# A two-layer attention trunk: wider value products for eight heads, one weight loaded earlier, two more products of ones, and scores kept negated

## The chip, the cores and the metric

The kernel runs on one core of a Trainium2 chip. The metric is the device time of one execution in microseconds (us). The kernel before took 671.21 us, the median of three runs (671.16, 671.21 and 672.38).

## The reference, cut to what matters

Two layers work on 512 tokens of 1024 numbers. Layer 0 mixes tokens by neighbourhood attention: 16 heads of 64 numbers, where a token sees a window of 8 x 16 tokens of a 64-wide grid. Layer 1 is a latent attention over all tokens. After each layer a gated embedding is added. All numbers are float32.

```
def mixer_na(xn, w_in, rpb, w_out):
    q, k, v, z = jnp.split(xn @ w_in, 4, axis=-1)
    o = neighbourhood_attention(q.reshape(shp), k.reshape(shp), v.reshape(shp), rpb)
    return (o.reshape(B, S, hd) * jax.nn.silu(z)) @ w_out
...
for i in range(DEPTH):
    xn = rmsnorm(x, norm_g[i])
    y = mixer_na(...) if i == 0 else mixer_mla(...)
    h = x + y
    gate = jax.nn.sigmoid(rmsnorm(h, ple_norm[i]) @ ple_w_gate[i])
    x = h + gate * (p[i] @ ple_w_proj[i])
return rmsnorm(x, final_norm)
```

## The kernel before

**Precision.** Every product of two float32 matrices is made of three products of rounded halves: high by high, low by high, high by low. So each operand exists as a pair: `hi`, a rounded copy that ScalarE (ACT) makes, and `lo`, the difference, which VectorE (DVE) or GpSimd (POOL) makes. `load_w` (L68) does this for a weight of 128 x 1024 numbers (512 KB): a DMA from SyncE's queue (SP) into `wraw`, the cast to `whi` on ACT (L78), the subtraction to `wlo` on POOL (L79). Each of the three names has three buffers that rotate, so the third load behind a product waits until that product has read its weight.

**The order of the work.** The program is recorded in the order of the code, and a scheduler that simulates the engines then sets the order in which each engine issues. On the chip each engine takes its instructions strictly in that order. The PSUM banks have four tags: `mm` (2 banks), `S` (2), `T` (3) and `O` (1).

**The start (`run`, L752 to L799).** TensorE (PE) first multiplies a matrix of ones by ones, `NWARM` = 9 times (L756); nothing reads the result. Then come the 48 products of the embedding of layer 0 (`ple`, L430 and L102), whose operands `ple_load` casts in halves of 512 columns (L409, L410). The first two z projections (`z_phase` with `ws`, L173) follow; their weights and the transposed x (`xT`) were loaded above. They are made from x without its row norm (`rh`, `rl`). The norm comes from the four row tiles of x, which are loaded (L783) and squared (L784); POOL takes the power (L787), PE turns it into rows (four transposes into `ps_T`, L128), and ACT copies it to `R` (L792). The third z weight is the first that goes through `load_w` (L790), behind the x tiles and six writes of embedding results (L445) in SP's queue. From the norm and `xT` DVE makes the normed x (L796), and its halves `xh` and `xl` (L797, L798) are the operands of all that follows.

**The heads of layer 0 (`na_heads`).** `project(j)` makes queries and keys of a pair of heads; for even j it first makes the values of four heads (L220 to L233): two weights, then for each of four token tiles 24 products of 256 columns into one `mm` bank, which `v_split` divides. `attend(j)` runs the two heads of a pair (`na_head`): score products (L318, L319); on DVE score plus bias with the row maximum beside it (L325, L328); the negation of the maximum (L332, 128 x 2 numbers, 32 times in all); exponentials on ACT (L336); reciprocal on DVE; the division on POOL (L341); seven blocks turned on PE (L352, L354); and the product with the values (L366). `project(j + 1)` is recorded ahead of `attend(j)`. The last three z projections come after the heads (L291).

Of the kernel before, what the change touches and what calls it, by code (L numbers as in the profile page):

```python
# [27 lines left out]
QSC = 96.0 ** -0.5  # L28
NWARM = 9
NLATE = 3  # L30
# [9 lines left out]
class Trunk:  # L40
# [27 lines left out]
    def load_w(self, ap, n, extra=False, parts=1, rest=None, late=None):  # L68

        nc = self.nc  # L70
        pool = self.wx if extra else self.wp
        raw = self.wp.tile([P, 1024], F32, name="wraw", tag="wraw", bufs=3)
        hi = pool.tile([P, n if extra else 1024], F32R, name="whi", tag="whi", bufs=self.wxn if extra else 3)
        lo = pool.tile([P, n if extra else 1024], F32R, name="wlo", tag="wlo", bufs=self.wxn if extra else 3)
        w = n // parts
        for c in [slice(i * w, (i + 1) * w) for i in range(parts)]:
            nc.sync.dma_start(raw[:, c], ap[:, c])
            self.last_cast = nc.scalar.activation(hi[:, c], raw[:, c], AF.Copy)  # L78
            f = lambda e, c=c: e.tensor_tensor(out=lo[:, c], in0=raw[:, c], in1=hi[:, c].bitcast(F32), op=ALU.subtract)  # L79
# [133 lines left out]
    def na_heads(self, pool, xT, zs, oT):  # L213
# [3 lines left out]
        V, A, U = {}, {}, {}  # L217

        def project(j):
            if j % 2 == 0:  # L220
                g = j // 2
                wv = [self.load_w(a["na_v"][g, c], 1024, rest=nc.vector if g == c == 0 else None) for c in range(2)]
                vts = V[g] = []
# [55 lines left out]
        for i in range(2):  # L279
            la = pool.tile([P, S], F32R, name=f"la{i}", bufs=1)  # L280
            lb = pool.tile([P, S], F32R, name=f"lb{i}", bufs=1)
            nc.gpsimd.memset(la[64:128].bitcast(F32), 0.0)
            nc.gpsimd.memset(lb[0:64].bitcast(F32), 0.0)
            self.rest_k.append((la, lb))
        last = project(0)
        for j in range(8):
# [9 lines left out]
    def na_head(self, pool, h, sq, s0, dk, kl, vh):  # L296
# [9 lines left out]
        for half in range(2):  # L306
# [13 lines left out]
            for i in range(2):  # L320
                qt = 2 * half + i
                c = slice(qt, qt + 1)
                if qt == 0:
                    for r, sc in ((slice(0, 64), slice(0, 128)), (slice(64, 128), slice(128, 256))):
                        nc.vector.tensor_tensor_reduce(out=ex[r, 0:P], in0=sp[r, sc], in1=bias[r, 0:P], scale=1.0,  # L325
                                                       scalar=NEG, op0=ALU.add, op1=ALU.max, accum_out=mx[r, c])
# [5 lines left out]
            nc.vector.tensor_scalar(mx[:, hs], mx[:, hs], -1.0, None, op0=ALU.mult)  # L332
# [411 lines left out]
    def run(self):  # L744
# [7 lines left out]
        with tc.tile_pool(name="pre", bufs=4, reuse_waits="tile") as pool:  # L752
            ones = [nc.const_aps.tensor(1.0, (P, n), mybir.dt.bfloat16) for n in (P, S)]
            ps = self.psum("T")
            for i in range(NWARM):
# [33 lines left out]
            R = pool.tile([P, S], F32, name="R", bufs=1)  # L789
            first = self.load_w(a["na_z"][2], 1024)  # L790
            with tc.issue_after(self.last_cast.ins):
                nc.scalar.activation(R, turned, AF.Copy)  # L792
            zs = self.z_phase(a["na_z"], raw, range(2), R=R, ws=ws)
            for k in range(KD):
# [3 lines left out]
                (nc.vector, nc.gpsimd)[k % 2].tensor_tensor(out=lo, in0=xs[k], in1=hi.bitcast(F32), op=ALU.subtract)  # L798
            zs.update(self.z_phase(a["na_z"], raw, range(2, 8 - NLATE), R=R, first=first))  # L799
        oT = ([self.bigtile(f"oh{g}") for g in range(2)], [self.bigtile(f"ol{g}") for g in range(2)])  # L800
# [90 lines left out]
def layouts(i):  # L891
# [20 lines left out]
    f["na_z"] = c(tiles(w[:, 3072:], P).reshape(8, P, 1024))  # L912
    f["na_v"] = c(tiles(w[:, 2048:3072], 256).reshape(4, P, 2, 1024).transpose(0, 2, 1, 3))

    def rows(w):
        return c(tiles(w, S).reshape(2, P, 4, 1024).transpose(0, 2, 1, 3))

    f["na_o"] = rows(i["na_w_out"][0])
    f["mla_o"] = rows(i["mla_w_out"][0])
# [61 lines left out]
```

## Time and profile before

| what | value |
|---|---|
| runs, median | 671.21 us |
| the profiled execution's own time | 672.45 us |
| its span, first to last instruction | 670.6 us |
| PE busy | 660.7 us, 99% |
| DVE, ACT, POOL busy | 367.8, 407.0, 392.7 us |
| matmuls on PE | 3561 |

A profile is one execution. Its rows give the start of a group of instructions in us from the start of the span, the busy time of the group, the engine, the line, the tile written and the tiles read, the shapes, and how many instructions were merged. Matmuls overlap, so the duration of one (0.39 us, say) is longer than the distance between two starts; it is the distance that counts on a full PE. PEld is PE's loading of the stationary operand, which runs beside the products.

### The profile page before, as it was taken

Reading aid. Unit: us, or ns where it says so; the run is one execution under the profiler, and the core shown is the slowest. Engines: PE = TensorE matmul, PEld = TensorE weight load, DVE = VectorE, ACT = ScalarE, POOL = GpSimd, SP = SyncE. Lnnn points to the kernel's source line nnn. Section 1 sums busy time; section 2 is a strip of 40 time slices with the busy share of each in tenths; the row PEclk is TensorE's granted clock in tenths of the full one; section 3 lists DMA queues with packets and bytes.
Section 4 is the critical chain, followed back from the end, with each engine's and each line's share of the span. In section 5 each row is a group of like instructions: output and inputs, shape, how many; then the busy total and the mean of one; then the engine's idle time right before and its main releaser. Section 6 shows DMA issues by size and latency. Waiting matters only on the chain.

```text
span 670.6 us, 10167 instructions
## 1 busy us (share of the span) xinstructions
PE 660.7 (99%) x3561; PEld 565.6 (84%) x3561; DVE 367.8 (55%) x827; ACT 407.0 (61%) x812; POOL 392.7 (59%) x321
## 2 busy tenths in 40 slices
PE   9999999999999999999999999999999999999995
PEld 6789898998988888888899887888888888888885
DVE  6371464646747624453624613888988875145234
ACT  6663765657767652653444535887989887436423
POOL 0295546666575565853044526786959786758411
PEclk9999999999999999999999999999999999999999
DMA  8843314223233127534143344120111222664122
GB/s 322 308 154 133 107 56 138 88 65 115 67 96 118 44 101 290 189 123 129 72 118 109 104 110 132 66 74 16 58 47 63 64 96 95 241 244 156 34 79 94
DMA packets 32387, 79.11 MB, mean 118 GB/s; under 512 B 4177, under 2 KB 8785, under 8 KB 32337
## 3 DMA queue, kind: packets, MB, share of 16 engines
q1 hardware_dynamic: 31904, 77.68, 35.1%
q10 hardware_dynamic: 432, 0.79, 0.3%
q8 instruction: 28, 0.46, 0.3%
q14 instruction: 23, 0.18, 0.1%
HBM read 66.92 MB, written 8.39 MB: 112 GB/s over the span
## 4 chain that ended last, share of the span: by engine, by line
PE 88%; DMA 5%; ACT 2%; DVE 2%; POOL 1%; issue 1%; SPq 0%; POOLq 0%; DVEq 0%; ACTq 0%
PE ps_mm L102 50%; PE ps_S L102 11%; PE ps_mm L534 6%; PE ps_T L128 6%; PE ps_O L645 4%; PE ps_T L102 3%; PE ps_O L102 2%; PE ps_O L366 2%; PE ps_T L354 1%; DMA wraw<-na_z 1%; PE ps_S L319 1%; PE ps_S L318 1%; DMA x<-x 1%; DMA wraw<-proj 1%; DMA xT<-xT 1%
## 5 line engine op out<-in xcount | busy, mean ns | idle before, releaser
L79 POOL TENSOR_TENSOR wlo<-wraw,whi 128x1024 fp32r<-128x1024 f32 (+5 forms) x106 | 207.7, 1976 | 103.5 <-ACT whi L78 85.2
L78 ACT ACTIVATE whi<-wraw 128x1024 fp32r<-128x1024 f32 (+5 forms) x108 | 93.2, 886 | 73.7 <-issue 18.1
L630 POOL TENSOR_TENSOR ex<-ex,rc 128x512 f32<-128x512 f32 x64 | 66.0, 1039 | 25.9 <-DVE rc L629 16.7
L102 PE MATMUL ps_mm<-whi,hnT 128*128 128x512 f32 (+1 forms) x272 | 70.2, 378 | 0.0
L102 PEld LDWEIGHTS ps_mm<-whi,hnT 128*128 128x128 f32 x272 | 49.3, 188 | 9.3
L341 POOL TENSOR_TENSOR ex<-ex,rc 128x128 f32<-128x128 f32 (+1 forms) x64 | 34.3, 560 | 38.0 <-DVE rc L337 36.4
L628 ACT ACTIVATE ex<-ps_S,mx 128x512 f32<-128x512 f32 x64 | 44.0, 688 | 12.5 <-DVE mx L626 11.3
L626 DVE TENSOR_REDUCE mx<-ps_S 128x1 f32<-128x512 f32 x64 | 43.7, 683 | 8.7 <-PE ps_S L102 7.9
L91 DVE TENSOR_TENSOR pt_lo<-ps_T,pt_hi 128x512 fp32r<-128x512 f32 x64 | 43.3, 682 | 7.6 <-ACT pt_hi L89 7.3
L336 ACT ACTIVATE ex<-ex,mx 128x128 f32<-128x128 f32 (+1 forms) x64 | 30.2, 473 | 21.8 <-DVE mx L332 21.4
L102 PE MATMUL ps_mm<-xh,whi 128*128 128x512 f32 x152 | 41.0, 400 | 0.1
L102 PE MATMUL ps_mm<-wlo,hnT 128*128 128x512 f32 (+1 forms) x136 | 40.5, 378 | 0.0
L89 ACT ACTIVATE pt_hi<-ps_T 128x512 fp32r<-128x512 f32 x64 | 37.7, 594 | 4.3 <-PE ps_T L128 4.0
L102 PE MATMUL ps_mm<-xh,wlo 128*128 128x512 f32 x152 | 39.2, 392 | 0.0
L102 PE MATMUL ps_mm<-xl,whi 128*128 128x512 f32 x152 | 38.7, 392 | 0.0
L128 PE MATMUL ps_T<-ident,ex 128*128 128x128 f32 x256 | 38.4, 272 | 0.0
L128 PEld LDWEIGHTS ps_T<-ident,ex 128*128 128x128 f32 x256 | 31.5, 140 | 7.7 <-POOL ex L630 0.4
L194 DVE TENSOR_TENSOR u<-ps_O,u 64x512 f32<-64x512 f32 x32 | 22.0, 686 | 23.1 <-ACT u L193 22.6
L102 PEld LDWEIGHTS ps_mm<-xl,whi 128*128 128x128 f32 x152 | 28.1, 188 | 5.7
L112 POOL TENSOR_TENSOR rs<-ss,half 128x1 f32<-128x1 f32 x20 | 12.7, 638 | 34.3 <-DVE ss L111 34.2
L102 PEld LDWEIGHTS ps_mm<-xh,wlo 128*128 128x128 f32 x152 | 28.1, 188 | 5.5
L464 DVE TENSOR_TENSOR sg<-pe,sg 128x512 f32<-128x512 f32 (+1 forms) x17 | 12.4, 728 | 36.1 <-ACT sg L463 36.1
(341 smaller groups left out, 1668.7 us busy)
## 6 DMA issues: line engine op xcount, KB each, us to landing
pe<-pe SPq DMA_DIRECT2D x32, 256.0 KB, 2.8
wraw<-na_qk SPq DMA_DIRECT2D x16, 512.0 KB, 3.3
wraw<-gate SPq DMA_DIRECT2D x16, 512.0 KB, 3.4
wraw<-na_v SPq DMA_DIRECT2D x8, 512.0 KB, 3.3
wraw<-na_o SPq DMA_DIRECT2D x8, 512.0 KB, 3.4
wraw<-mla_z SPq DMA_DIRECT2D x8, 512.0 KB, 3.6
wraw<-mla_o SPq DMA_DIRECT2D x8, 512.0 KB, 3.6
wraw<-na_z SPq DMA_DIRECT2D x6, 512.0 KB, 6.2
```

What stands on the lines that cost most here:

```text
L78: self.last_cast = nc.scalar.activation(hi[:, c], raw[:, c], AF.Copy)
L79: f = lambda e, c=c: e.tensor_tensor(out=lo[:, c], in0=raw[:, c], in1=hi[:, c].bitcast(F32), op=ALU.subtract)
L89: self.last_copy = nc.scalar.activation(hi, src, AF.Copy, scale=scale)
L91: nc.vector.tensor_tensor(out=lo, in0=src, in1=hi.bitcast(F32), op=ALU.subtract)
L102: last = self.last_mm = nc.tensor.matmul(out, l, r, start=i == 0, stop=i == n - 1)
L128: self.last_mm = self.nc.tensor.transpose(t[:, i * P:(i + 1) * P], b, self.ident)
L336: self.last_exp = nc.scalar.activation(e, e, AF.Exp, bias=mx[:, qt:qt + 1], accum_out=sm[:, qt:qt + 1])
L341: nc.gpsimd.tensor_tensor(out=e, in0=e, in1=rc[:, qt:qt + 1].to_broadcast([P, e.shape[1]]), op=ALU.mult)
L534: self.last_mm = nc.tensor.matmul(PS[key], *terms[i], start=i == 0, stop=i == len(terms) - 1)
L626: nc.vector.reduce_max(mx, sp, axis=AX.X, negate=True)
L628: nc.scalar.activation(ex, sp, AF.Exp, bias=mx, accum_out=sm)
L630: nc.gpsimd.tensor_tensor(out=ex, in0=ex, in1=rc.to_broadcast([P, S]), op=ALU.mult)
```

## The change

Four things change.

- `NWARM` goes from 9 to 11.
- A new function `values` makes the values of the first eight heads ahead of `project(0)`. It loads four weights (`na_v0`, each 256 rows of the weight by 512 columns), keeps four PSUM banks open (three `T` and the one `O`), and adds to all four for each weight. It makes 96 products of 512 columns; `project(0)` and `project(2)` made 192 of 256 columns. The results go through `v_split` as before, in the same eight pieces. `project(4)` and `project(6)` make the other eight heads' values as before.
- The third z weight is loaded between the second and third row tile of x, cast on ACT, and its low half made on POOL. The rule that held `R` back behind the cast of that weight is gone.
- Scores of layer 0 are kept negated: the DVE instruction multiplies score plus bias by -1 and takes the minimum, and ACT's exponential has a scale of -1. The negation of the maximum is left out.

In the first `values` weight the low half is made by POOL; in the first weight of the values before, DVE made it (`rest`).

```
-NWARM = 9
+NWARM = 11
...
+        def values():
+
+            pss = [self.psum(b) for b in ("T", "T", "T", "O")]
+            for c in range(4):
+                w = self.load_w(a["na_v0"][c], 1024)
+                for i, (s, r) in enumerate(((0, 0), (1, 0), (0, 1))):
+                    for kt, ps in enumerate(pss):
+                        for k in (2 * c, 2 * c + 1):
+                            nc.tensor.matmul(ps, X((xh, xl)[s], k, kt), w[r][:, k % 2 * S:(k % 2 + 1) * S],
+                                             start=k == 0 and i == 0, stop=k == KD - 1 and i == 2)
+            for g in range(2):
+                V[g] = [pool.tile([P, S], F32R, name="vt", tag="vt", bufs=8) for kt in range(NT)]
+            for kt, ps in enumerate(pss):
+                for g in range(2):
+                    self.v_split(V[g][kt], ps[:, g * 256:(g + 1) * 256])
+
         def project(j):
-            if j % 2 == 0:
+            if j in (4, 6):
                 g = j // 2
-                wv = [self.load_w(a["na_v"][g, c], 1024, rest=nc.vector if g == c == 0 else None) for c in range(2)]
+                wv = [self.load_w(a["na_v1"][g - 2, c], 1024) for c in range(2)]
...
+        values()
         last = project(0)
...
-                                                   in1=bias[:, P:], scale=1.0, scalar=NEG, op0=ALU.add, op1=ALU.max,
+                                                   in1=bias[:, P:], scale=-1.0, scalar=-NEG, op0=ALU.add, op1=ALU.min,
                                                    accum_out=mx[:, c])
             hs = slice(2 * half, 2 * half + 2)
-            nc.vector.tensor_scalar(mx[:, hs], mx[:, hs], -1.0, None, op0=ALU.mult)
...
-                self.last_exp = nc.scalar.activation(e, e, AF.Exp, bias=mx[:, qt:qt + 1], accum_out=sm[:, qt:qt + 1])
+                self.last_exp = nc.scalar.activation(e, e, AF.Exp, scale=-1.0, bias=mx[:, qt:qt + 1],
+                                                     accum_out=sm[:, qt:qt + 1])
...
-                   for n, d in (("wraw", F32), ("whi", F32R), ("wlo", F32R))] for _ in range(2)]
+                   for n, d in (("wraw", F32), ("whi", F32R), ("wlo", F32R))] for _ in range(3)]
+            first = ws.pop()
...
             for t in range(NT):
+                if t == 2:
+                    nc.sync.dma_start(first[0], a["na_z"][2])
                 nc.sync.dma_start(xt[t], a["x"][t])
                 nc.scalar.activation(xt[t], xt[t], AF.Square, accum_out=ss[:, t:t + 1])
...
-            first = self.load_w(a["na_z"][2], 1024)
-            with tc.issue_after(self.last_cast.ins):
-                nc.scalar.activation(R, turned, AF.Copy)
+            nc.scalar.activation(first[1], first[0], AF.Copy)
+            nc.gpsimd.tensor_tensor(out=first[2], in0=first[0], in1=first[1].bitcast(F32), op=ALU.subtract)
+            nc.scalar.activation(R, turned, AF.Copy)
             zs = self.z_phase(a["na_z"], raw, range(2), R=R, ws=ws)
```

The scheduler moves more than the diff shows, so the order itself is given at three places. In these rows a line, an operation, the tile written and the tiles read stand in the order of issue; from line 219 on, line numbers of the changed program are up to 21 higher.

**PE at the third z weight.** `L173` are the first two z projections, `ps_S<-rh` and `ps_S<-rl` the third with the fourth behind it, and the four transposes of `ssq` are the norm on its way to `R`. Before:

```order
L173 MATMUL ps_mm<-rh_133,wlo 128x512 x2
L128 MATMUL ps_T<-ident,ssq 128x128 x4
L102 MATMUL ps_S<-rh_132,whi 128x512 x4
L102 MATMUL ps_S<-rh_133,whi 128x512 x4
L102 MATMUL ps_S<-rl_134,whi 128x512 x4
L102 MATMUL ps_S<-rl_135,whi 128x512 x4
```

After:

```order
L173 MATMUL ps_mm<-rh_135,wlo 128x512 x2
L102 MATMUL ps_S<-rh_134,whi 128x512 x4
L102 MATMUL ps_S<-rh_135,whi 128x512 x4
L102 MATMUL ps_S<-rl_136,whi 128x512 x4
L102 MATMUL ps_S<-rl_137,whi 128x512 x3
L128 MATMUL ps_T<-ident,ssq 128x128 x4
L102 MATMUL ps_S<-rl_137,whi 128x512
```

The transposes moved behind 15 products of the third z projection.

**PE at the values.** Before, `ps_mm<-whi,xh` and its like are the values of heads 0 to 3, of which the last of four token tiles and the query product behind it are shown:

```order
L102 MATMUL ps_mm<-whi,xh_136 128x256 x4
L102 MATMUL ps_mm<-whi,xh_137 128x256 x4
L102 MATMUL ps_mm<-whi,xl_138 128x256 x4
L102 MATMUL ps_mm<-whi,xl_139 128x256 x4
L102 MATMUL ps_mm<-wlo,xh_136 128x256 x4
L102 MATMUL ps_mm<-wlo,xh_137 128x256 x4
L102 MATMUL ps_mm<-xh_136,whi 128x512 x4
```

After, the products of one of the four weights stand in six rows, from the end of the fifth z projection on:

```order
L102 MATMUL ps_mm<-rh_135,wlo 128x512 x4
L227 MATMUL ps_T<-whi,xh_138 128x512 x6
L227 MATMUL ps_O<-whi,xh_138 128x512 x2
L227 MATMUL ps_T<-whi,xl_140 128x512 x6
L227 MATMUL ps_O<-whi,xl_140 128x512 x2
L227 MATMUL ps_T<-wlo,xh_138 128x512 x6
L227 MATMUL ps_O<-wlo,xh_138 128x512 x2
```

All values of eight heads now stand at this place, ahead of the first queries; before, those of heads 4 to 7 stood between the scores of heads 0 to 3.

**POOL around the power of the norm (`ssq`).** `wlo` are low halves of weights, `xl` those of the normed x. Before:

```order
L787 TENSOR_TENSOR ssq<-ssq,half 128x4
L79 TENSOR_TENSOR wlo<-wraw,whi 128x1024 x3
L798 TENSOR_TENSOR xl_138<-xT,xh_136 128x512 x2
L798 TENSOR_TENSOR xl_139<-xT,xh_137 128x512 x2
L79 TENSOR_TENSOR wlo<-wraw,whi 128x1024 x2
```

After:

```order
L811 TENSOR_TENSOR wlo<-wraw,whi 128x1024
L806 TENSOR_SCALAR ssq<-ssq 128x4
L807 TENSOR_TENSOR ssq<-ssq,half 128x4
L79 TENSOR_TENSOR wlo<-wraw,whi 128x1024 x3
L818 TENSOR_TENSOR xl_140<-xT,xh_138 128x512 x2
L818 TENSOR_TENSOR xl_141<-xT,xh_139 128x512
L79 TENSOR_TENSOR wlo<-wraw,whi 128x1024
L818 TENSOR_TENSOR xl_141<-xT,xh_139 128x512
L79 TENSOR_TENSOR wlo<-wraw,whi 128x1024
```

The third z weight's low half now stands ahead of the power, and the weights of the values stand between the low halves of x.

More of the change, by code (lines that the diff above doesn't have):

```diff
@@ L77, in load_w @@
             nc.sync.dma_start(raw[:, c], ap[:, c])
-            self.last_cast = nc.scalar.activation(hi[:, c], raw[:, c], AF.Copy)
+            nc.scalar.activation(hi[:, c], raw[:, c], AF.Copy)
             f = lambda e, c=c: e.tensor_tensor(out=lo[:, c], in0=raw[:, c], in1=hi[:, c].bitcast(F32), op=ALU.subtract)
@@ L324, in na_head @@
                     for r, sc in ((slice(0, 64), slice(0, 128)), (slice(64, 128), slice(128, 256))):
-                        nc.vector.tensor_tensor_reduce(out=ex[r, 0:P], in0=sp[r, sc], in1=bias[r, 0:P], scale=1.0,
-                                                       scalar=NEG, op0=ALU.add, op1=ALU.max, accum_out=mx[r, c])
+                        nc.vector.tensor_tensor_reduce(out=ex[r, 0:P], in0=sp[r, sc], in1=bias[r, 0:P], scale=-1.0,
+                                                       scalar=-NEG, op0=ALU.add, op1=ALU.min, accum_out=mx[r, c])
                 else:
                     nc.vector.tensor_tensor_reduce(out=ex[:, ecol(qt)], in0=sp[:, i * 256:(i + 1) * 256],
-                                                   in1=bias[:, P:], scale=1.0, scalar=NEG, op0=ALU.add, op1=ALU.max,
+                                                   in1=bias[:, P:], scale=-1.0, scalar=-NEG, op0=ALU.add, op1=ALU.min,
                                                    accum_out=mx[:, c])
             hs = slice(2 * half, 2 * half + 2)
-            nc.vector.tensor_scalar(mx[:, hs], mx[:, hs], -1.0, None, op0=ALU.mult)
             for i in range(2):
@@ L798, in run @@
                 (nc.vector, nc.gpsimd)[k % 2].tensor_tensor(out=lo, in0=xs[k], in1=hi.bitcast(F32), op=ALU.subtract)
-            zs.update(self.z_phase(a["na_z"], raw, range(2, 8 - NLATE), R=R, first=first))
+            zs.update(self.z_phase(a["na_z"], raw, range(2, 8 - NLATE), R=R, first=first[1:]))
         oT = ([self.bigtile(f"oh{g}") for g in range(2)], [self.bigtile(f"ol{g}") for g in range(2)])
@@ L912, in layouts @@
     f["na_z"] = c(tiles(w[:, 3072:], P).reshape(8, P, 1024))
-    f["na_v"] = c(tiles(w[:, 2048:3072], 256).reshape(4, P, 2, 1024).transpose(0, 2, 1, 3))
+    f["na_v1"] = c(tiles(w[:, 2560:3072], 256).reshape(2, P, 2, 1024).transpose(0, 2, 1, 3))
     def rows(w):
         return c(tiles(w, S).reshape(2, P, 4, 1024).transpose(0, 2, 1, 3))
+    f["na_v0"] = c(tiles(w[:, 2048:2560], S).reshape(P, 4, 1024).transpose(1, 0, 2))
     f["na_o"] = rows(i["na_w_out"][0])
```

## The prediction

> **What bounds the kernel now.** I read first the page's busy times (us, share of the span, instructions) and, for later, the rate of the DMA engines in 40 equal slices:
>
> ```profile
> PE 660.7 (99%) x3561; PEld 565.6 (84%) x3561; DVE 367.8 (55%) x827; ACT 407.0 (61%) x812; POOL 392.7 (59%) x321
> GB/s 322 308 154 133 107 56 138 88 65 115 67 96 118 44 101 290 189 123 129 72 118 109 104 110 132 66 74 16 58 47 63 64 96 95 241 244 156 34 79 94
> ```
>
> PE is full and the other engines are at some 60%. A full PE says little by itself, so next comes the view of waits, for PE alone (who waited for whom, us in total, times, longest):
>
> ```profile
> PE ps_T L756 <- PEq L970: 0.8, 1, 0.8
> PE ps_mm L430 <- ACT whi L409: 0.6, 1, 0.6
> PE ps_S L102 <- ACT whi L78: 0.6, 1, 0.6
> PE ps_S L102 <- DMA qe<-rl: 0.5, 2, 0.3
> ```
>
> These are all: 2.5 us in 670.6. So the end is set by the sum of PE's intervals, one matmul behind the other. What takes work from ACT, DVE, POOL or a queue gains nothing, unless it ends one of these waits; what shortens PE's own sequence gains in full, as long as no new wait appears.
>
> **Values.** The timeline of PE gives the interval from one matmul to the next, if starts of rows are subtracted. The rows are the first and last of heads 0 to 3's values, the first of the three query and key products behind them (nine rows of 8 matmuls), and the first score:
>
> ```profile
> 46.65 1.12 PE L102 MATMUL ps_mm<-whi,xh 128*128 128x256 f32 x8
> ...
> 57.20 1.12 PE L102 MATMUL ps_mm<-wlo,xh 128*128 128x256 f32 x8
> 58.16 2.00 PE L102 MATMUL ps_mm<-xh,whi 128*128 128x512 f32 x8
> ...
> 74.51 0.28 PE L318 MATMUL ps_S<-da,s 128*128 128x256 f32 x1
> ```
>
> 96 products of 256 columns took 58.16 - 46.65 = 11.51 us, 0.1199 each; 72 of 512 columns took 74.51 - 58.16 = 16.35 us, 0.2271 each. The change removes 192 of the first (23.02 us) and adds 96 of the second (21.80 us): **-1.22 us**. The wide product is not half price, since two narrow ones cost 0.240; that is why 96 fewer matmuls are worth so little. Loads stay four of 512 KB, and `v_split` keeps its eight casts and eight subtractions of 256 columns, beside the next products as before. The operands have more time than before: a weight now feeds 24 x 0.227 = 5.45 us of PE. POOL is the slowest supplier (its rows, and one of DVE):
>
> ```profile
> 30.22 7.16 POOL L79 TENSOR_TENSOR wlo<-wraw,whi 128x1024 fp32r<-128x1024 f32 x3 [5.72 <-ACT whi L78]
> 37.34 6.85 POOL L798 TENSOR_TENSOR xl<-xT,xh 128x512 fp32r<-128x512 f32 x4
> ...
> 31.87 5.35 DVE L796 SCALAR_TENSOR_TENSOR xT<-ps_T,g,xT 128x512 f32<-128x512 f32 x8
> ```
>
> 2.39 us per weight and 1.71 per `xl`. In its new order POOL has, from about 30.2: three weights (the third is the values' first, done near 37.4), three `xl` (42.5), the second weight (44.9), an `xl` (46.6), the third weight (49.0). The values start near 44.4 (46.65 less the two terms below); they read low halves of weight one 16 products in (48.0), of weight two at 53.5, of weight three at 58.9, and the last `xl` near 62. The smallest distance is over 8 us. The values' third `T` bank is the one that DVE reads eight times for the normed x (5.35 us): before it was free at 37.2, now the norm comes some 2 us later. Cost 0; the bound above is one late weight, 2.4 us.
>
> **Third z weight.** Here PE waits, for a weight that lands late. The rows are from PE's and ACT's timelines, from the chain of work (the load of the third x tile, issue to landing), and from POOL's timeline (the power); the last two are PE's again, four transposes without a wait:
>
> ```profile
> 29.04 0.60 PE L128 MATMUL ps_T<-ident,ssq 128*128 128x128 f32 x4
> 30.20 2.11 PE L102 MATMUL ps_S<-rh,whi 128*128 128x512 f32 x8 [0.56 <-ACT whi L78]
> ...
> 29.09 1.06 ACT L78 ACTIVATE whi<-wraw 128x1024 fp32r<-128x1024 f32 x1 [5.03 <-DMA wraw<-na_z]
> ...
> 13.31 6.74 DMA x<-x
> ...
> 23.48 1.02 POOL L787 TENSOR_TENSOR ssq<-ssq,half 128x4 f32<-128x4 f32 x1
> ...
> 238.32 0.60 PE L354 MATMUL ps_T<-ident,ex 128*128 128x128 f32 x4
> 238.67 0.48 PE L102 MATMUL ps_mm<-xh,whi 128*128 128x512 f32 x1
> ```
>
> From the transposes to the next product 1.16 us, elsewhere 0.35: **-0.81 us** if the weight is there. It now stands where the third x tile stood, which landed at 20.05. ACT had nothing to do from 24.06 on (29.09 less 5.03), so even behind all of ACT's earlier work the cast (1.05) ends by 25.1 and POOL's low half (2.4) by 27.5; PE needs the cast at 29.04 less the next term, 27.6, and the low half 16 products later. What moves back: two x tiles by one transfer, 1.6 us (512 KB at 322 GB/s, an estimate), and the power behind the low half. It ends by 28.7 at the latest, instead of 24.5. The transposes that read it now stand 15 products later (27.6 + 15 x 0.227 = 31.0). `R` and the normed x come 3.4 us later relative to PE, which the values read 12 us later. Bounds: -0.81, and 0 if the weight is as late as before.
>
> **Eleven products of ones.** The start of PE's timeline shows two speeds, and DVE's and ACT's show when the operands arrive:
>
> ```profile
> 0.77 4.00 PE L756 MATMUL ps_T<-const-bfloat16-1.0 128*128 128x512 bf16 x9 [0.77 <-PEq L970]
> 5.38 0.80 PE L430 MATMUL ps_mm<-whi 128*128 128x512 f32 x1 [0.62 <-ACT whi L409]
> ...
> 6.41 0.63 PE L430 MATMUL ps_mm<-whi,wlo 128*128 128x512 f32 x1
> ...
> 8.54 0.63 PE L102 MATMUL ps_S<-whi 128*128 128x512 f32 x1
> ...
> 9.28 0.39 PE L102 MATMUL ps_S<-whi 128*128 128x512 f32 x1
> 9.51 0.40 PE L102 MATMUL ps_S<-wlo,whi 128*128 128x512 f32 x1
> ...
> 4.84 1.29 DVE L410 TENSOR_TENSOR wlo<-wraw,whi 128x512 fp32r<-128x512 f32 x2 [3.98 <-ACT whi L409]
> 6.57 2.67 DVE L410 TENSOR_TENSOR wlo<-wraw,whi 128x512 fp32r<-128x512 f32 x4 [0.43 <-ACT whi L409]
> ...
> 7.23 1.29 ACT L409 ACTIVATE whi<-wraw 128x512 fp32r<-128x512 f32 x2 [0.17 <-DMA wraw<-proj]
> ```
>
> From 6.41 to 8.54 (five intervals) a product starts every 0.426 us, from 9.28 on every 0.23. The nine ones end near 4.7, PE is idle until 5.38, and the full clock (0.23) comes some 3.7 us after PE begins again. Eleven ones from 0.77 on last to 0.77 + 11 x 0.426 = 5.46: the gap is filled, and the first real product starts 0.08 us later. If the gap is what kept PE slow, the full clock comes before 6. Then the third product is bound by DVE's second low half (4.84 + 1.29 = 6.13, so 6.2), and the seven up to the one that started at 9.28 take 0.23 each: 7.8. That is 1.48 earlier. The supply follows: ACT's last cast ends at 8.52 and the first product that needs it would start near 9.4; the last low half ends at 9.24 and is needed near 12. The z weights' last halves end here, and the products that follow the first half of their terms started there:
>
> ```profile
> 19.30 1.29 DVE L777 TENSOR_TENSOR wlo<-wraw,whi 128x512 fp32r<-128x512 f32 x2
> ...
> 23.38 0.41 PEld L173 LDWEIGHTS ps_mm<-rh,whi 128*128 128x128 f32 x2
> ```
>
> 20.59 against 23.38 - 1.48 = 21.9, so 1.3 us are left. Bounds: +0.08 if the full clock comes at 9.1 all the same; -1.6 if all eight slow intervals are saved. I take **-1.45 us**. [...]
>
> **Negated scores.** 32 DVE instructions go, of this group, and the last of them stood in the way of the only wait that the heads show. The rows are the group (taken over 70 to 240 us) DVE, ACT and PE near the end of the heads, and PE at the same pair of kinds earlier:
>
> ```profile
> L332 DVE TENSOR_SCALAR mx<-mx 128x2 f32<-128x2 f32 x32 | 15.2, 489 | 0.4
> ...
> 230.81 1.98 DVE L332 TENSOR_SCALAR mx<-mx 128x2 f32<-128x2 f32 x1
> ...
> 236.17 1.09 ACT L163 ACTIVATE z<-ps_mm 128x512 f32<-128x512 f32 x2
> ...
> 236.47 0.27 PE L352 MATMUL ps_T<-ident,ex 128*128 128x128 f32 x1
> 236.82 1.66 PE L102 MATMUL ps_mm<-xh,whi 128*128 128x512 f32 x6
> ...
> 82.61 0.27 PE L352 MATMUL ps_T<-ident,ex 128*128 128x128 f32 x1
> 82.64 0.48 PE L102 MATMUL ps_mm<-whi,xh 128*128 128x256 f32 x2
> ```
>
> DVE's 15.2 us are off the path. But PE's z product at 236.82 started 0.35 us behind a transpose, against 0.03 at 82.61: its bank came free with ACT's first z of the two, which stands on ACT behind the last exponentials, and these waited for 1.98 us of negation. Without it they are over a microsecond earlier: **-0.3 us** (bounds 0 and -0.32). The scale of -1 in the exponential costs nothing by the nearest rows: a copy of 64 x 512 with a scale of 0.125 (L239) and one without (L257) both took 0.59 us:
>
> ```profile
> 63.83 0.59 ACT L239 ACTIVATE sa<-ps_mm 64x512 fp32r<-64x512 f32 x1 [0.70 <-PE ps_mm L102]
> ...
> 69.27 0.59 ACT L257 ACTIVATE da<-ps_mm 64x512 fp32r<-64x512 f32 x1 [0.70 <-PE ps_mm L102]
> ```
>
> **The sum.** -1.22 - 0.81 - 1.45 - 0.3 = -3.8 us. The profiled execution took 672.45 us (span 670.6), so 668.65 for such a one. The median of the runs is 671.21, 1.24 below; carried over, **667.5 us** (-0.56%).
>
> **Rivals.**
>
> - *The ones bring nothing.* The full clock comes when it did, or the median run already had it early: the runs lie at 671.2 and 672.4, and 1.2 us between them is near the 1.48 of that term. For it: 3.9 us without a gap did not open the clock, 3.7 later did, so length alone doesn't decide. Then -2.3: 668.9 to 669.1. Chance 0.24.
> - *A part is eaten by new waits in layer 0.* All values come first, so the scores start later and the order of every engine is new. Transposes of the first head stand one product behind its pair's scores instead of six narrow ones, 0.5 us less. Waits like those of before, 0.3 to 0.8 us each, two to four of them: 668.2 to 670.7. Against it: exponentials come earlier without the negation. Chance 0.12.
> - *Slower: the heads become the bound.* Scores began at 74.51. Now 11.5 - 1.2 us more stand ahead of them, less 2.3 gained: 82.5; and the phase should end 3.8 earlier. So 16 heads have about 154 us instead of 165, 9.6 each instead of 10.3. Two `ex` buffers let two heads run at once. The first head's scores began at 74.51 and its first block was turned at 82.61; with the other six blocks it held its buffer for some 10 us, and the point from which this decides is 2 x 9.6 = 19.2. To lose 0.2% beyond the gain of 3.8 it would have to cost 5.2 us, 0.33 a head: 673 to 675. Against it: this factor of nearly two. Chance 0.04.
> - *The value products don't get cheaper,* since with fp32r halves and four open banks a product takes over 0.24 instead of 0.227; then this term is 0 or above: 668.7 to 669.5. Against it: the 72 of the same shape and types above. Chance 0.04.
>
> **How the numbers follow.** My forecast has 0.56 (666.9 to 668.2). The range for 8 in 10 reaches down to all bounds together (-1.22 - 0.81 - 1.6 - 0.32 = -3.95, and 0.5 for the spread of runs: 666.8) and up over the first rival and most of the second: 666.8 to 669.8. A measurement of this kernel can tell 0.2%, 1.34 us, from no change; that is 669.87. Faster needs the forecast, the first rival, the last, and half of the second: 0.88. Same 0.08, slower 0.04.
>
> **What would show it.** In the changed profile: the value products at 0.227 us from start to start, from near 44 to 66; no wait of PE for the third z weight, and the transposes of `ssq` behind 15 products; products at 0.23 us from about 6 on instead of 9.3; PE's waits down to the start and the two for `qe`; 3467 matmuls, 94 fewer. I am wrong if the slow interval of 0.42 still holds near 8, if PE shows waits between 44 and 240, or if the median lies above 669.8.

## The result, and the profile after

The changed kernel took **668.11 us** (median of six runs, 667.82 to 668.29), the kernel before, run beside it, 671.27 (six runs, 671.12 to 672.38): 3.16 us less, a ratio of 0.995 with an interval of [0.9938, 0.9963]. The forecast was 667.5.

The page of the profile after gives the busy times, and the share of each engine in the chain that ended last:

```profile
PE 657.2 (99%) x3467; PEld 560.1 (84%) x3467; DVE 354.3 (53%) x794; ACT 408.7 (61%) x812; POOL 394.8 (59%) x322
...
PE 94%; POOL 1%; ACT 1%; DMA 1%; issue 1%; DVE 1%; POOLq 0%; DVEq 0%; ACTq 0%
```

3467 matmuls, 94 fewer, and PE as full as before. The view of waits, PE alone, whole:

```profile
PE ps_T L773 <- PEq L991: 0.8, 1, 0.8
PE ps_S L102 <- DMA qe<-rl: 0.3, 1, 0.3
PE ps_mm L447 <- ACT whi L426: 0.3, 1, 0.3
```

The wait for the third z weight is gone, and the two for `qe` are one. PE's timeline at the start (start, busy time, line, tiles, shapes):

```profile
0.77 4.06 PE L773 MATMUL ps_T<-const-bfloat16-1.0 128*128 128x512 bf16 x11 [0.77 <-PEq L991]
5.11 0.50 PE L447 MATMUL ps_mm<-whi 128*128 128x512 f32 x1 [0.28 <-ACT whi L426]
...
5.92 0.50 PE L447 MATMUL ps_mm<-whi,wlo 128*128 128x512 f32 x1
6.26 0.39 PE L447 MATMUL ps_mm<-whi 128*128 128x512 f32 x1
6.49 0.39 PE L447 MATMUL ps_mm<-wlo,whi 128*128 128x512 f32 x1
```

From 6.26 on a product starts every 0.23 us. Eleven ones did not last until 5.46 as estimated but until 4.8, since the full clock came in the midst of them, at 3.89, when eight of them had started. PE's timeline at the third z weight, the values and the late heads, and at the first product of the norm behind layer 0's mixer (`x1h`):

```profile
27.36 1.98 PE L102 MATMUL ps_S<-rh,whi 128*128 128x512 f32 x8
29.18 1.75 PE L102 MATMUL ps_S<-rl,whi 128*128 128x512 f32 x7
30.77 0.60 PE L128 MATMUL ps_T<-ident,ssq 128*128 128x128 f32 x4
...
44.16 1.52 PE L227 MATMUL ps_T<-whi,xh 128*128 128x512 f32 x6
...
65.92 1.98 PE L102 MATMUL ps_mm<-xh,whi 128*128 128x512 f32 x8
...
82.24 0.28 PE L335 MATMUL ps_S<-da,s 128*128 128x256 f32 x1
...
233.66 0.27 PE L369 MATMUL ps_T<-ident,ex 128*128 128x128 f32 x1
233.69 0.48 PE L102 MATMUL ps_mm<-xh,whi 128*128 128x512 f32 x1
...
327.83 0.51 PE L102 MATMUL ps_mm<-whi,x1h 128*128 128x384 f32 x2
```

The third z products follow without a wait, the four transposes stand behind 15 of them. The 96 value products took 65.92 - 44.16 = 21.76 us, 0.2267 each. The late transpose has 0.03 us behind it where it had 0.35. The same last mark of the kernel before:

```profile
332.12 0.51 PE L102 MATMUL ps_mm<-whi,x1h 128*128 128x384 f32 x2
```

These marks cut the span into three stretches, which serve for all that follows: the **start** (up to the first product behind the z phase), the **values and heads** (from there to `x1h`), and the **rest**. Before: 46.65, 285.47 and 338.47 (to 670.6). After: 44.16, 283.67 and 338.20 (to 666.0). So the profiled executions differ by 2.49 + 1.80 + 0.27 = 4.56 us. The profiled execution of before (672.45) is among its longer ones and that of after (667.82) is its shortest, which is why the medians differ by less.

### The profile page after: what moved, and what is told of

It reads as the page before. It is cut to its first block, busy times and chain, and to the rows that moved or that the text cites. A ratio compares the mean times of both kernels' runs of the same rounds, so it can differ in the third digit from the quotient of the medians.

```text
span 666.0 us, 9965 instructions
## 1 busy us (share of the span) xinstructions
PE 657.2 (99%) x3467; PEld 560.1 (84%) x3467; DVE 354.3 (53%) x794; ACT 408.7 (61%) x812; POOL 394.8 (59%) x322
## 4 chain that ended last, share of the span: by engine, by line
PE 94%; POOL 1%; ACT 1%; DMA 1%; issue 1%; DVE 1%; POOLq 0%; DVEq 0%; ACTq 0%
PE ps_mm L102 48%; PE ps_S L102 12%; PE ps_mm L551 6%; PE ps_T L128 6%; PE ps_O L662 4%; PE ps_T L102 3%; PE ps_O L102 3%; PE ps_T L227 2%; PE ps_O L383 2%; PE ps_mm L173 2%; PE ps_T L371 2%; PE ps_S L336 1%; PE ps_S L335 1%; PE ps_O L227 1%; POOL ex L647 1%
```

## The experiments

Twelve kernels ran in three groups, each group on a chip of its own (e1 to e4; e0 and e5 to e7; e8 to e11). Each ratio is to the runs of the kernel before in the same group (medians 671.67, 672.09 and 671.92); where kernels of different groups are compared, it is the ratios that count. "Clock" is the moment at which the trace's record of the granted clock goes to full. The stretches are of the one profiled execution of each.

| kernel | median | ratio, interval | clock | start | values, heads | rest |
|---|---|---|---|---|---|---|
| before | 671.27 | 1 | 9.13 | 46.65 | 285.47 | 338.47 |
| after | 668.11 | 0.995 [0.9938, 0.9963] | 3.89 | 44.16 | 283.67 | 338.20 |
| e0, after again | 668.39 | 0.9945 [0.9931, 0.9958] | 3.90 | 44.39 | 283.69 | 338.63 |
| e1, nine ones | 668.43 | 0.9951 [0.9939, 0.9964] | 3.85 | 44.39 | 283.63 | 338.83 |
| e4, late z weight | 668.36 | 0.995 [0.9938, 0.9962] | 5.20 | 44.33 | 283.63 | 338.78 |
| e6, both of these | 670.0 | 0.9969 [0.9957, 0.998] | 9.29 | 46.42 | 283.64 | 338.46 |
| e7, four ones | 670.07 | 0.9971 [0.9959, 0.9982] | 10.10 | 46.23 | 283.63 | 338.44 |
| e8, fifteen ones | 669.14 | 0.9955 [0.9943, 0.9968] | 5.80 | 45.06 | 283.68 | 338.70 |
| e3, narrow values | 676.59 | 1.0075 [1.0062, 1.0089] | 4.65 | 44.56 | 291.69 | 338.91 |
| e5, negations back | 669.84 | 0.9967 [0.9955, 0.998] | 6.22 | 44.40 | 284.71 | 338.69 |
| e11, negations unread | 669.13 | 0.9956 [0.9944, 0.9969] | 4.09 | 44.34 | 284.09 | 338.65 |
| e2, before + ones | 670.27 | 0.9977 [0.9968, 0.9986] | 5.08 | 44.42 | 285.43 | 338.24 |
| e9, before + negated | 671.84 | 0.9996 [0.9988, 1.0005] | 10.13 | 46.87 | 284.96 | 339.26 |
| e10, before + wide | 671.22 | 0.9992 [0.9983, 1.0001] | 5.09 | 45.66 | 284.65 | 339.11 |

The middle column hardly varies from execution to execution (after, e0, e1, e4, e6, e7 and e8, which have the same heads, lie within 0.06 us; before and e2 within 0.04), so one profile is enough to read it. The start does vary, with the clock: 44.16 to 45.66 where it came by 6.22, 46.23 to 46.87 where it came at 9.13 or later.

### The start: e1, e2, e4, e6, e7, e8, and after again

e0 is the changed kernel itself. e1 undoes the ones in it, e2 puts them alone into the kernel before:

```
-NWARM = 11
+NWARM = 9
```

```
-NWARM = 9
+NWARM = 11
```

e4 is the changed kernel with the third z weight loaded as before:

```
...
-                if t == 2:
-                    nc.sync.dma_start(first[0], a["na_z"][2])
...
-            nc.scalar.activation(first[1], first[0], AF.Copy)
-            nc.gpsimd.tensor_tensor(out=first[2], in0=first[0], in1=first[1].bitcast(F32), op=ALU.subtract)
-            nc.scalar.activation(R, turned, AF.Copy)
+            first = self.load_w(a["na_z"][2], 1024)
+            with tc.issue_after(self.last_cast.ins):
+                nc.scalar.activation(R, turned, AF.Copy)
...
```

e6 makes the edits of e1 and e4 both. e7 and e8 are the changed kernel with four and with fifteen ones:

```
-NWARM = 11
+NWARM = 4
```

```
-NWARM = 11
+NWARM = 15
```

> The changed kernel with nine products of ones again, all else as changed. Theory A (the idle gap after nine ones keeps the clock slow in nearly every execution): median 669.4 to 669.7, 1.3 to 1.6 us above the changed kernel. [...] In the profile, where PE's products start every 0.43 us until after 8, the first z product starts near 18; where they start every 0.23 us from before 6, near 16.5.

> The kernel before with eleven products of ones and nothing else changed. Theory A: 669.7 to 669.9, 1.4 us below before. [...] The wait for the third z weight stays and is longer by what the start gained, since its load has not moved: 0.6 us before, then up to 2.

> The changed kernel with the third z weight loaded behind the x tiles and the writes of the embedding, as before. If its landing is what PE waits for: a wait of PE for the cast of this weight comes back, 0.8 us plus what the start gains on average (0.8 to 1.5), so 669.0 to 670.4. Rival, that the moved transposes hide it: 668.1 to 668.4.

> The changed kernel with nine products of ones and the third z weight loaded late, so only the wide values and the negated scores are changed. Each of the two alone could be undone without loss. Theory C (either of them removes the wait for the third z weight: the early load by itself, the two ones because the scheduler then puts this load ahead of the sixth embedding write): both undone bring the wait back, 0.5 to 2 us in PE's waits, and the median is 1.0 to 2.2 above the changed kernel, 669.1 to 670.5. Theory D (neither is needed once the values are wide): within 0.5 of the changed kernel.

> The changed kernel with four products of ones, which end near 2.5 us and leave PE idle until 5.1 to 5.4. Gap theory (a long gap keeps the clock slow): products start every 0.43 us until 8.6 to 12 in every execution, and the time is 1.3 to 3 us above the changed kernel, 669.4 to 671. Rival (the ones do not matter to the clock): within 0.4 of it.

> The changed kernel with fifteen matmuls of ones instead of eleven. The ones would end at about 5.6 instead of 4.7 us, past the 5.1 to 5.35 at which the first product starts, so PE has no idle time after them and the first product starts 0.2 to 0.4 later. Theory gap (an idle stretch before the first product can delay the full clock): no later opening in any execution, so a narrower spread, median 668.2 to 668.8. If even the 0.3 to 0.5 of idle time that eleven ones leave costs something in the usual execution: below 668.1. If the extra ones only delay the work: 668.6 to 668.8.

> The changed kernel once more, unchanged, as the measure for the other runs of this group: 668.0 to 668.6.

**One of the two edits removes the wait.** Nine ones alone cost nothing that can be measured (e1), the late load alone nothing (e4), both together 1.6 us (e6 against e0). Neither e2 nor e4 shows PE waiting for the third z weight. These rows of e2's timeline show why, SP's issues of loads and writes first, then ACT's cast of the weight and PE:

```profile
15.26 2.47 SPq L445 DMA_DIRECT2D pe<-pe  x4
18.64 0.33 SPq L77 DMA_DIRECT2D wraw<-na_z  x1
19.98 0.32 SPq L445 DMA_DIRECT2D pe<-pe  x1
...
26.60 1.06 ACT L78 ACTIVATE whi<-wraw 128x1024 fp32r<-128x1024 f32 x1 [2.64 <-DMA wraw<-na_z]
...
27.63 0.60 PE L128 MATMUL ps_T<-ident,ssq 128*128 128x128 f32 x4
27.99 2.09 PE L102 MATMUL ps_S<-rh,whi 128*128 128x512 f32 x8
```

(The row of four writes leaves out the first one, at 14.58, so five stand ahead of the load.) In the kernel before SP issues six writes of the embedding first:

```profile
14.73 4.43 SPq L445 DMA_DIRECT2D pe<-pe  x6
20.07 1.64 SPq L77 DMA_DIRECT2D wraw<-na_z  x2
```

With two more products of ones the scheduler, which simulates the engines, places the load ahead of the last of the six writes, at 18.64 instead of 20.07; in e4 it is at 18.83. The weight lands in time: the cast begins at 26.60 instead of 29.09. So e2's 1.40 us are not the clock's alone: an edit at PE's head moved a DMA 18 us later. In e10 and e6, which have neither edit, all six writes stand ahead of the load (20.01 and 19.86), and the weight lands late. PE's timeline of e10, clock at 5.09:

```profile
29.20 2.11 PE L102 MATMUL ps_S<-rh,whi 128*128 128x512 f32 x8 [1.21 <-ACT whi L78]
```

And of e6, clock at 9.29:

```profile
29.96 1.43 PE L102 MATMUL ps_S<-rh,whi 128*128 128x512 f32 x5 [0.30 <-ACT whi L78]
```

More than half of what an early clock gains is taken back there: e10's start is 45.66, e6's 46.42, 0.76 apart, while their first products of the z phase stand 1.66 apart (16.52 and 18.18).

The early load does not make up for a late clock, though. e7 has the early load and the clock at 10.10, and its start is 1.84 later than e0's. In e6's profiled execution the start is 2.03 later than e0's, and 1.46 of this is there at the first product of the z phase already. So e1 ties with the changed kernel because the clock came early in its profile and, as far as their times tell, in its other runs.

**The clock.** PE's timeline of e7, four ones:

```profile
0.77 1.86 PE L773 MATMUL ps_T<-const-bfloat16-1.0 128*128 128x512 bf16 x4 [0.77 <-PEq L991]
5.33 0.80 PE L447 MATMUL ps_mm<-whi 128*128 128x512 f32 x1 [2.69 <-ACT whi L426]
...
9.76 0.56 PE L102 MATMUL ps_S<-wlo,whi 128*128 128x512 f32 x1
10.15 0.40 PE L447 MATMUL ps_mm<-wlo,whi 128*128 128x512 f32 x1
```

With a gap of 2.69 us products start 0.43 apart until the clock comes at 10.10, and the time is 1.7 us longer; in before, with a gap of 0.62, it came at 9.13. With eleven ones, seven profiles have the clock between 3.89 and 6.22 (after, e0, e2, e3, e4, e5, e11), with fifteen e8 at 5.80. With nine, five profiles have it at 3.85, 5.09, 9.13, 9.29 and 10.13. So no profile with eleven has a late clock, and two of the five with nine have an early one. In the profile after it was not the two extra ones that opened it: eight ones had started by 3.89, and e1's nine had it at 3.85. In e5's profile the clock came at 6.22, behind eleven ones that lasted until 5.6 with no wait of PE after them; that the two extra ones count in executions like this one is an estimate, which no run shows. e1's five runs (668.08 to 668.68) show no sign of a late clock. Five are few: e10's eleven runs fall into seven from 670.54 to 671.62 and four from 672.02 to 672.44. Fifteen ones only delay the first product, to 6.29, and cost 0.67 in the start.

Of what was expected, e6 and e7 came out by their first theories (theory C, and the gap), though e6's wait is 0.3 us and not 0.5 or more. e1's median, 668.43, is some 1 us below what its theory A gives. e2's is 1.40 below before's (670.27 against 671.67), as its theory A has it, but the wait that was to stay was gone. e4 fits its rival, but the transposes had not moved there; the order on SP did it. e8 is slower than all three of its theories.

### The values: e3 and e10

e3 is the changed kernel with the narrow values back:

```
-        def values():
...
-            if j in (4, 6):
+            if j % 2 == 0:
...
-                wv = [self.load_w(a["na_v1"][g - 2, c], 1024) for c in range(2)]
+                wv = [self.load_w(a["na_v"][g, c], 1024, rest=nc.vector if g == c == 0 else None) for c in range(2)]
...
-        values()
...
```

e10 puts the same lines the other way round into the kernel before, and nothing else.

> The changed kernel with the values of the first eight heads as before, in 192 products of 256 columns at their old places. By the intervals (0.1199 against 0.2271 us) 1.2 us above the changed kernel: 669.3. Rival, that the new order of the heads costs or saves something of its own: off from 669.3 by 0.4 or more.

> The kernel before with the first eight heads' values in products of 512 columns, and nothing else (nine ones, third z weight as before, negations as before). The value products alone should be worth 1.2 us by their durations. If the parts add up: wide values with negated scores were 670.0 with before at 672.09, so 2.1 together; less 1.4 for the negated scores leaves 0.7 to 1.2, which is 670.4 to 671.4, ratio 0.998 to 0.999. If the narrow values had been limited by the supply of xl in before too, as they were in the changed kernel, the gain would be over 2 us: under 669.8. In the profile: 96 value products at 0.227, PE's wait for the third z weight as in before or longer.

e3 is 8 us slower than the changed kernel instead of 1.2. Its largest wait:

```profile
PE ps_mm L102 <- DVE xl L801: 3.6, 3, 2.3
```

The three places in PE's timeline:

```profile
46.10 0.50 PE L102 MATMUL ps_mm<-whi,xl 128*128 128x256 f32 x2 [0.19 <-DVE xl L801]
47.77 0.50 PE L102 MATMUL ps_mm<-whi,xl 128*128 128x256 f32 x2 [1.17 <-DVE xl L801]
50.53 0.80 PE L102 MATMUL ps_mm<-whi,xl 128*128 128x256 f32 x2 [2.25 <-DVE xl L801]
```

And the view by stretches (start:end, length, busy time of PE, PEld, DVE, ACT and POOL with instructions, granted clock, DMA's share and GB/s):

```profile
42.00:49.00 7.00, 4.92 (x27) 3.83 (x25) 7.00 (x4) 1.46 (x2) 7.00 (x4) 1.00 0.45 151
49.00:56.00 7.00, 5.47 (x26) 5.47 (x27) 3.10 (x4) 1.61 (x3) 2.99 (x5) 0.51 0.50 156
```

The narrow products take a token tile at a time and need all eight `xl` within 2 us; the wide ones take a pair of `xl` per weight and need the last near 62. DVE's timeline shows why four of them are late, e3 first, then the kernel before:

```profile
39.51 2.03 DVE L79 TENSOR_TENSOR wlo<-wraw,whi 128x1024 fp32r<-128x1024 f32 x1
41.45 9.02 DVE L801 TENSOR_TENSOR xl<-xT,xh 128x512 fp32r<-128x512 f32 x4
...
37.13 5.89 DVE L798 TENSOR_TENSOR xl<-xT,xh 128x512 fp32r<-128x512 f32 x4
```

They end 7.5 us later than in before. The normed x, behind the moved transposes, accounts for 1.8 (33.64 against 31.87). Another 2.6 are one z product's eviction and the first weight's low half, which DVE makes ahead of them in e3 and behind them in before. The last 3.1 are the four subtractions themselves: two of them run beside a weight's low half on POOL and take 2.8 to 2.9 us; the two beside an `xl` on POOL take some 1.8. And PE reads them 2.1 earlier (44.56 against 46.65). So the moved transposes are only a part of it. PE waits 3.6 us, and the clock is at half from 49.03 to 55.85 (0.51 in the second stretch above). From 51.12 to 54.54 16 products start 0.214 us apart, against 0.12 at full clock; at that pace the time from the end of the last wait (50.53) to 55.85 costs some 2.3 us more, an estimate. With the products' 1.2 this is 7.1 of the 8 us; the rest is not traced. The rival, an order with a price of its own, is what came out.

In the kernel before no such wait was there, so alone the wide values gain little: e10's middle stretch is 0.82 shorter than before's, not 1.26. PE waits 0.3 there for a norm near the end of layer 0 (below). Its median, 671.22, is in the expected range, but its interval reaches to no change.

### The negations: e5, e11 and e9

e5 puts the negations back into the changed kernel:

```
...
-                                                   in1=bias[:, P:], scale=-1.0, scalar=-NEG, op0=ALU.add, op1=ALU.min,
+                                                   in1=bias[:, P:], scale=1.0, scalar=NEG, op0=ALU.add, op1=ALU.max,
...
+            nc.vector.tensor_scalar(mx[:, hs], mx[:, hs], -1.0, None, op0=ALU.mult)
...
-                self.last_exp = nc.scalar.activation(e, e, AF.Exp, scale=-1.0, bias=mx[:, qt:qt + 1],
-                                                     accum_out=sm[:, qt:qt + 1])
+                self.last_exp = nc.scalar.activation(e, e, AF.Exp, bias=mx[:, qt:qt + 1], accum_out=sm[:, qt:qt + 1])
```

e11 adds to the changed kernel the DVE instruction alone, into a tile that nobody reads:

```
+        dm = self.small.tile([P, 4], F32, name="dm", tag="dm")
...
+            nc.vector.tensor_scalar(dm[:, hs], mx[:, hs], -1.0, None, op0=ALU.mult)
```

e9 puts the lines of e5, the other way round, into the kernel before.

> The changed kernel with scores kept as before: the 32 negations on DVE are back and the exponential has no scale. If they stood in the way of one wait near the end of the heads only: 0.2 to 0.4 us above the changed kernel. Rival, that they are on no path now that the order is new: within 0.15 of it.

> The changed kernel with a negation of the row maxima put back at its old place on the DVE, into a tile that nobody reads; the exponentials take the unnegated bias as in the changed kernel. The DVE has the old load, the chain from scores to exponentials does not wait for it. Theory chain (what costs is that the exponential waits for the negation): about 668.4, as the changed kernel. Theory occupancy (what costs is the DVE's 13 to 15 us of negations, which hold up the evictions behind them): about 669.8, as with the negations back. By the program's order the scheduler may place other work differently, so 0.3 either way is not told apart.

> The kernel before with the first layer's scores kept negated, and nothing else. The prediction took 0.3 us for this part; putting the negations back into the changed kernel cost 1.45 us (669.84 against 668.39). Theory A (the part is worth about 1.4 us wherever it stands, since the negations lengthen the chain of every head on the DVE): about 670.3 to 670.8, ratio 0.997 to 0.9985. Rival (0.3 as predicted; the 1.45 came from the order that the changed kernel had around layer 0's end): about 671.4 to 672, ratio 0.999 to 1.0.

The negations cost 1.45 us in e5 (669.84 against e0's 668.39), far more than either of its two expectations, and 1.02 of it is in the middle stretch of the two profiles. The view of one line in e5, the negation of `mx` (durations min/median/max in ns, first and last start, and further down who waited for it, us and times):

```profile
L349 DVE TENSOR_SCALAR mx<-mx x32: 147/169/1398, 86.6 to 229.6; 128x2 f32<-128x2 f32 x32
...
  ACT ex L353: 15.8, 14
```

The timelines of POOL, DVE and ACT in e5 at the first head:

```profile
90.19 2.40 POOL L79 TENSOR_TENSOR wlo<-wraw,whi 128x1024 fp32r<-128x1024 f32 x1
...
91.23 1.45 DVE L349 TENSOR_SCALAR mx<-mx 128x2 f32<-128x2 f32 x2
...
92.65 0.40 ACT L353 ACTIVATE ex<-ex,mx 128x128 f32<-128x128 f32 x1 [0.49 <-DVE mx L349]
```

In e5 this instruction on two numbers per partition takes 0.17 us at the median, and up to 1.4. The one at 91.23 (the first of the two in the row) ended at 92.61, and POOL's low half of a weight at 92.59. The long ones all ended so: in five profiles with negations (before, e2, e5, e10, e11) 52 of 160 took over 0.3 us, and each of the 52 ended 21 to 33 ns behind the end of a POOL instruction; none of the short ones lies inside one. So the exponential that reads `mx` then starts behind the end of a POOL instruction. Not every DVE instruction is held so: the 160 reciprocals of the same five profiles, also on 128 x 2 numbers, took 0.14 to 0.17 us, and 43 of them lie inside a POOL instruction. Why the negation is held and the reciprocal is not, no run shows; the longest negation took 2.1 us (in before).

How the 1.02 divides: at 222.55 in e0 PE has made as many products of each kind since the start of the values as at 222.95 in e5 and at 222.66 in e11. Counted from the start of the values, e5 has lost 0.39 by then, nearly all of it by 122.65; the view of waits shows none of it, and PE's order there is another than e0's. e11 has lost 0.16. At the first output product of the heads (`oh`) e5 is 0.41 behind and e11 0.45, but most of e11's comes from one place just ahead of it. PE's timeline of e0, then of e11:

```profile
226.75 0.30 PE L383 MATMUL ps_O<-ph,vt 128*128 128x256 f32 x1
226.88 0.69 PE L102 MATMUL ps_S<-whi,oh 128*128 128x512 f32 x2
...
226.87 0.30 PE L385 MATMUL ps_O<-ph,vt 128*128 128x256 f32 x1
227.28 0.70 PE L102 MATMUL ps_S<-whi,oh 128*128 128x512 f32 x2
```

0.41 us from one to the next, against 0.13. So the DVE instruction without the chain costs something too (its time, or the order that came with it), 0.40 in the middle stretch, but not where e5 loses it. By its ratio e11 lies about halfway between e0 and e5: neither of its two theories holds alone. Whether e5's early loss comes from the exponentials' wait, from DVE's time or from the order that the scheduler made stays open. Behind `oh` e11 loses no more; e5 loses another 0.6, most of it around a wait that e11 hasn't. Here is its line in the view of waits of e5:

```profile
PE ps_T L128 <- DVE ss L111: 0.4, 1, 0.4
```

And its place in PE's timeline, a norm's transposes that wait for a sum of squares:

```profile
288.27 0.63 PE L128 MATMUL ps_T<-ident,hg 128*128 128x128 f32 x4 [0.37 <-DVE ss L111]
```

e10 has the same wait, of 0.3. These are the two kernels with wide values and negations on the chain; no other shows it. Why it comes so long after the last negation (229.6) was not tried; DVE's order ahead of it differs from e0's.

In e9 the middle stretch is 0.51 shorter than in before; 0.32 of it is the delay between a transpose and a z product that the prediction named (0.35 in before, 0.03 in e9). In e10 and e5, which have negations and wide values, that delay is 0.03 too: the new order of the heads takes it away by itself. But the rest of e9 is 0.79 longer. Its longest wait:

```profile
PE ps_S L102 <- DMA qe<-rl: 1.4, 2, 0.8
```

In before this line was 0.5. The median (671.84, the kernel before 671.92) agrees with no gain, as the rival of e9 had it. Whether that longer wait is chance or comes with the earlier heads stays open: the rest varies from 338.20 to 339.26 over the profiles.

## Why the prediction was right, point by point

- **What bounds.** Right. The losses of the twelve runs that could be traced are waits, a slow clock, more ones or another order on PE. DVE's 13.5 us less busy time are worth far less than 13.5 (e11: 0.40 in the middle stretch).
- **Values, -1.22.** The term was right: 21.76 us against 23.02. The supply was judged rightly for the new order. Two things were not seen: that the narrow order could not have borne the late `xl` (e3), and that alone the new order brings a wait (e10).
- **Third z weight, -0.81.** The wait went and the transposes moved behind 15 products, as said. But the term does not belong to this edit alone: the two ones already move the load (e2, e4). By e6 against e1 and e4 either of the two removes the wait. Which of them has the credit in the changed kernel is a matter of counting: in the two profiled executions the start gained 2.49, and 1.68 of it stands at the first z product already, which leaves 0.81.
- **Ones, -1.45.** In the two profiled executions the first z product came 1.68 us earlier (18.16 to 16.48), since the clock came during the ones. That is partly luck: it came at 3.89, and e1 had it at 3.85 with nine ones. The first z of e10 at 16.52, with nine ones and an early clock, suggests that in other executions of the kernel before there was nothing to gain at this mark. For the start 2.26 was forecast and 2.49 came, a little beyond both bounds together (2.41): the first real product started 0.27 earlier (5.11 instead of 5.38), not 0.08 later. Where before's clock is early, its start would be about e10's 45.66 and the gain 1.3 to 1.5 (an estimate from e10, e0 and after), because the late weight had taken the rest.
- **Negated scores, -0.3.** This term was too small in the changed kernel: 1.45 in the medians (e5 against e0). The delay behind 236.47 went, as said, but e5, with its negations, does not have it either. The step that does not hold is "DVE's 15.2 us are off the path": even in e11, where nothing waits for the result, the instruction, or the order that comes with it, costs 0.40 in the middle stretch. In e5 it is 1.02, with negations up to 1.4 us long and exponentials waiting 15.8 us for them; how much of that is the wait and how much the order is not shown. In before's order the negations are worth 0.51 in the middle stretch (e9) and nothing in the median.
- **The sum.** For the middle stretch -1.52 was predicted and -1.80 came. The parts alone give -0.82 (e10) and -0.51 (e9), 1.33, though both hold the 0.32 of the delay; the other 0.47 comes only when both are made, and the wait for the norm is a part of it. For the start -2.26 was taken from one execution and carried to the median unchanged. By e10's start the median execution offered some 1.3 to 1.5 there, and 1.4 + 1.8 = 3.2 is near what the medians show (3.16). By this estimate the start fell short of its term by some 0.8 us and the middle gave 0.3 more.
- **The chances.** The forecast, the first and the last rival and half of the second add up to 0.90 for faster, not 0.88.
- **Rivals.** The first, that the median run had the clock early already, may be half true. No profile of the kernel before shows an early clock, but e10's does, with the same order at the start and 671.22 us. The gain did not fall to 2.3 all the same; e10 shows a reason, since its early start met a longer wait for the third z weight (1.21). New waits in the heads did not come (the scores began at 82.24, and 82.5 was forecast), so the heads did not become the bound, and the products kept 0.227.

None of the twelve is faster than the changed kernel; e1 and e4 tie with it.

## What to carry to other kernels

Where the start depends on a clock that opens at a varying moment (here 3.85 to 10.13 us), take terms from several executions, or from marks behind the first fixed event (here a landing weight), not from one. A duration with a mean far above its median (in before 0.489 against 0.17 us) hid a wait here: look at what ends with it, and at an instruction of the same shape that does not wait. Two kernels that are equally far behind at one mark need not have lost it in the same place: follow them back to where the difference arose. Undo an edit's parts one at a time and do them one at a time: here two edits each removed the same wait, and a third part (the wide values) made the lateness of `xl` harmless.

## What the runs showed of the hardware

The granted clock went to full between 3.85 us (e1) and 10.13 us (e9) in the 14 profiles. In before products start 0.426 us apart ahead of that moment (9.13) and 0.23 behind it. One and the same start of the program did not give the same moment: before and e10, with nine ones and the same order of the start, had it at 9.13 and 5.09. In before and after the clock then stayed full until 667.90 and 662.66, behind the end of PE's last product (663.26 and 658.70). Only in e3 did it fall within the work: to half at 49.03, inside the longest of PE's three waits for `xl` (2.25 us, up to 50.53), and back to full at 55.85. What sets these moments no run shows.
